# Layer 2's shift and scale as VectorE sums, attention's list in a new order, scaling shared with GpSimd

## The chip, the cores and the metric

The kernel runs on one core of a Trainium2 chip. The engines that matter are TensorE (PE, with its weight loads as PEld), VectorE (DVE), ScalarE (ACT), GpSimd (POOL) and SyncE (SP), which issues most of the loads. Each engine takes its instructions in order and waits on semaphores for the others. The metric is the device time of one execution in microseconds, as the median of several runs; beside it stands one execution that the hardware profiler recorded.

## The reference

Two layers on 256 tokens of width 1024, in float32. Each layer is `x + gate * mixer(rmsnorm(x, g) * (1 + scale) + shift)`, and shift, scale and gate are thirds of one product with the condition vector c (1024 numbers):

```
for i in range(DEPTH):
    shift, scale, gate = jnp.split(c @ ada_w[i] + ada_b[i], 3, axis=-1)
    h = rmsnorm(x, norm_g[i]) * (1.0 + scale[:, None, :]) + shift[:, None, :]
    y = nsa_mixer(h, ...) if i == 0 else mlstm_mixer(h, ...)
    x = x + gate[:, None, :] * y
return rmsnorm(x, final_g)
```

Layer 1's mixer is sparse attention: 16 heads in 4 groups, a compressed, a selected and a sliding branch (with 256 tokens the selected and the sliding branch see all earlier tokens), each a softmax with a distance bias, weighted by sigmoid gates, multiplied by a SiLU path z and projected by w_out. Layer 2's mixer is a chunkwise mLSTM. Shift and scale of layer 2, 2 x 1024 sums over the 1024 entries of c, are what the change computes in another way. They depend on c and weights alone and are needed first when layer 2 begins.

## The kernel before

**Stages.** The opening norms the tokens, makes layer 1's shift and scale and projects the queries and the compression inputs (up to about 50 us); eight blocks of key, value and gate weights follow (to 71 us); then come the attention (71 to about 158 us), its output projection with the residual, the norm of layer 2 (the boundary, `turn`, to about 195 us), and layer 2.

**Weights.** All weights go through one queue: `add` enters a block, `_load_one` issues its DMA on SP, in the queue's order, into one of ten buffers called raw. A block's buffer is free for the tenth block behind it once it was used. Weights that TensorE multiplies are split into two float32r parts, the high part by ACT (`make_hi`, L162) and the rest by DVE (`make_lo`, L167), the steps `hi` and `lo`; others (kind None) are used as they are, through `take_raw`.

**The attention's list.** Between 71 and 158 us nothing is left to a scheduler. `ORDER` is a text of some 300 steps, and each engine gets its instructions in the order in which the steps issue them. A step names its kind and numbers. n = 0 to 7 counts pairs of key groups: four heads i = n // 2, two group pairs n % 2.

- `S:n,a` scores on PE (L770, L773), `m:n,a` adds distances and takes minima on DVE (L787, out of PSUM into a tile Pr), `e:n,a` exponentials on ACT (L794), `f:n` factors from sums and gates on DVE (L800 to L802).
- `s:n,j` and `p:n,j` scale the four pieces of one Pr by the factors (L808), s on DVE, p on POOL; `T:n,j,br` turns a third of them on PE (L813), `t:n,j,br` copies the turned ones on ACT (L641, into PT), `V:n` multiplies by the values on PE (L830), `C:i` adds the compressed branch (L835), `y:i` multiplies by z on DVE (L839), `Y:i` splits that in two (ACT L641, DVE L843).
- `z:n,q` are quarters of the SiLU path's products (L1598 to L1600), `zt`, `zo` its tanh and product; `hidden:n`, `gelu`, `turned`, `second`, `ckeys`, `cscores`, `cexp` and others are the compressed branch; `gr`, `gc`, `gs`, `ga` layer 1's gate.
- `cr:n` makes a quarter of layer 2's shift and scale as rows: 32 small matmuls on PE (`ada_rows`, L224), which leave four partial sums on four rows per 32 partitions; `cc` copies them out of PSUM on ACT; `cs` (`ada_sums`) turns the copy by four transposes on PE (L1617), adds the four parts on DVE (L1620) and applies bias and norm weight (L1627, L1628). Three quarters stand in the list, the fourth in `turn` at the boundary.

In the opening, layer 1's own shift and scale are made another way: `columns` (L416) multiplies a block of 128 weight rows, laid out with the outputs on partitions, by a broadcast c (`cbc`, 128x1024) on DVE and sums along the row in the same instruction.

**The boundary.** `turn` finishes the output projection (L878, last parts), applies the residual (`residual`, L1070 and L1071), squares on ACT (L1106), makes the root (`rms_rsqrt`, L207 to L212), scales (L1110, L1111), turns the rows (`transposed`, L1120) and applies shift and scale (`modulate`, L1130, L1132).

Of the kernel before, what the change touches and what calls it, by code (L numbers as in the profile page):

```python
# [23 lines left out]
class Kernel:  # L24
# [223 lines left out]
    def setup(self):  # L248
# [25 lines left out]
        c = self.compress = self.T(self.p1, [P, 704])  # L274
# [12 lines left out]
        self.dc = self.T(self.p1, [P, 2, 4, 4, 16])  # L287
        slopes = self.T(self.p1, [P, 16])
# [32 lines left out]
    def layer1(self):  # L321
# [32 lines left out]
        for n in range(4):  # L354
            hidden(n)

        def gate_path(ih, gp):
            for k in range(2):
                self.add("z", [P, 4, 2, 128], t["path"][4 * ih + 2 * gp + k])

        self.gate_path = gate_path
# [8 lines left out]
    def first_phase(self, place):  # L370
# [8 lines left out]
        self.cbc = self.T(pc, [P, D], tag="gate")  # L379
# [59 lines left out]
        def parameters():  # L439
            nc.vector.tensor_scalar(pca[:, 80:88], pca[:, 80:88], 1.0, None, op0=OP.add)  # L440
# [120 lines left out]
    def nsa(self, acc):  # L561
# [4 lines left out]
        self.gate0, self.cols1 = self.T(pc, [P, D], tag="gate"), []  # L566
# [56 lines left out]
    hi hidden:0 bias hi hidden:1 S:0,0 S:0,1 hidden:2 lo m:0,0 e:0,0 hidden:3 m:0,1 lo e:0,1 gelu:0 f:0 gelu:1 S:1,0 s:0,0 gelu:2 z:0,0 z:0,1 s:0,1 params  # L623
    T:0,0,0 hi T:0,0,1 turned S:1,1 m:1,0 t:0,0,0 second t:0,0,1 z:0,2 T:0,1,0 e:1,0 z:0,3 ckeys m:1,1 t:0,1,0 e:1,1 cvalues:0 cscores:0 lo cscores:1 zt:0
    f:1 p:1,0 T:0,1,1 cvalues:1 ccopy:0 S:2,0 ccopy:1 t:0,1,1 S:2,1 V:0 m:2,0 T:1,0,1 T:1,0,0 ctokens:0 e:2,0 zo:0 m:2,1 t:1,0,1 cdist:0 ctokens:1 t:1,0,0
    hi cdist:1 cexp z:1,0 e:2,1 p:1,1 T:1,1,1 lo cprobs z:1,1 cparts:0 cparts:1 T:1,1,0 z:1,2 z:1,3 S:3,0 zt:1 t:1,1,0 f:2 S:3,1 t:1,1,1 m:3,0 s:2,0
    cturned:0 zo:1 cpt:0 e:3,0 V:1 cturned:1 C:0 m:3,1 y:0 T:2,0,1 t:2,0,1 T:2,0,0 t:2,0,0 p:2,1 gr:0 cpt:1 T:2,1,0 T:2,1,1 e:3,1 t:2,1,0 t:2,1,1 gc:0 f:3
    S:4,0 gr:1 s:3,1 V:2 m:4,0 gs:0 s:3,0 ga:0 gc:1 hi S:4,1 T:3,0,1 m:4,1 T:3,0,0 gs:1 hi hi ga:1 t:3,0,1 t:3,0,0 T:3,1,1 e:4,0 lo e:4,1 T:3,1,0 t:3,1,0
    S:5,0 m:5,0 hi f:4 p:4,0 t:3,1,1 S:5,1 s:4,1 C:1 z:2,0 z:2,1 m:5,1 e:5,0 lo cr:0 V:3 T:4,0,1 z:2,2 T:4,0,0 t:4,0,1 e:5,1 T:4,1,1 z:2,3 y:1 t:4,0,0
    cc:0 lo f:5 t:4,1,1 zt:2 T:4,1,0 t:4,1,0 S:6,0 S:6,1 m:6,0 zo:2 V:4 s:5,0 m:6,1 T:5,0,0 p:5,1 z:3,0 e:6,0 T:5,0,1 e:6,1 t:5,0,1 lo cs:0 f:6 t:5,0,0  # L630
    z:3,1 cr:1 Y:0 T:5,1,0 T:5,1,1 cc:1 s:6,1 S:7,0 t:5,1,1 S:7,1 s:6,0 t:5,1,0 V:5 m:7,1 T:6,0,1 T:6,0,0 z:3,2 hi e:7,1 z:3,3 m:7,0 lo cs:1 e:7,0 t:6,0,0
    t:6,0,1 T:6,1,0 f:7 zt:3 zo:3 C:2 t:6,1,0 hi hi y:2 T:6,1,1 t:6,1,1 cr:2 cc:2 hi V:6 cs:2 lo out:0 lo root s:7,1 Y:1 hi out:1 lo p:7,0 lo hi lo Y:2
    """

    def attention(self, hidden_block):
# [31 lines left out]
        def turned():  # L667
# [3 lines left out]
            hk = W["hk"] = T([P, 2, 64])  # L671
            hv = W["hv"] = T([P, 2, 4, 2, 16])
# [131 lines left out]
        def scaled(n, j, e):  # L804
# [878 lines left out]
```

## Time and profile before

| | |
|---|---|
| median of 3 runs | 436.75 us (436.2 to 436.87) |
| profiled execution, own time | 436.06 us |
| its span in the trace | 434.0 us |
| mean granted TensorE clock | 0.997 |
| attention, weights of layer 2's shift and scale | 16 loads of 512 KB |

The page of the profile has six parts: busy time by engine, the span in 40 slices, DMA queues, the chain of work that ended last, the costliest groups of instructions and the DMA issues. Besides it the trace answers queries: busy times in windows, groups by line, what an engine waited for, the chain in order of time, and a timeline. In a group's row, `x128 | 7.7, 382 | 0.0` is the count, the busy time in us, the mean of one in ns, and the idle time ahead; a row of the timeline or the chain starts with its start and its length in us; a row of waits ends with the sum, the number and the longest. "DVE y L658 <- PE bank L590" reads: DVE's instruction of line 658, which writes a tile y, waited for PE's of line 590, which wrote a bank of PSUM.

### The profile page before, as it was taken

Reading aid. Unit: us, or ns where it says so; the run is one execution under the profiler, and the core shown is the slowest. Engines: PE = TensorE matmul, PEld = TensorE weight load, DVE = VectorE, ACT = ScalarE, POOL = GpSimd, SP = SyncE. Lnnn points to the kernel's source line nnn. Section 1 sums busy time; section 2 is a strip of 40 time slices with the busy share of each in tenths; the row PEclk is TensorE's granted clock in tenths of the full one; section 3 lists DMA queues with packets and bytes.
Section 4 is the critical chain, followed back from the end, with each engine's and each line's share of the span. In section 5 each row is a group of like instructions: output and inputs, shape, how many; then the busy total and the mean of one; then the engine's idle time right before and its main releaser. Section 6 shows DMA issues by size and latency. Waiting matters only on the chain.

```text
span 434.0 us, 7874 instructions
## 1 busy us (share of the span) xinstructions
PE 425.4 (98%) x2864; PEld 365.7 (84%) x2864; DVE 336.5 (78%) x751; ACT 272.7 (63%) x544; POOL 37.5 (9%) x92
## 2 busy tenths in 40 slices
PE   8999999999999999999999999999999999999994
PEld 4999998888688777888999899988888888888883
DVE  5999897889677596879985497889887977458554
ACT  6665785777976974659476765564466455455522
POOL 4000302152032200120000000000000000000000
PEclk9999999999999999999999999999999999999998
DMA  8999986931875698638764456638555867540002
GB/s 325 416 415 418 401 264 190 400 143 51 311 297 191 251 337 271 243 97 267 267 189 151 148 164 198 203 131 275 194 153 194 277 248 218 182 136 0 2 0 97
DMA packets 26886, 94.55 MB, mean 218 GB/s; under 512 B 3072, under 2 KB 3088, under 8 KB 26848
## 3 DMA queue, kind: packets, MB, share of 16 engines
q1 hardware_dynamic: 26208, 92.30, 60.8%
q10 hardware_dynamic: 288, 0.79, 0.7%
q0 software_dynamic: 352, 0.97, 0.7%
q8 instruction: 22, 0.36, 0.3%
q14 instruction: 16, 0.13, 0.1%
HBM read 93.00 MB, written 1.05 MB: 217 GB/s over the span
## 4 chain that ended last, share of the span: by engine, by line
PE 94%; DVE 2%; DMA 1%; ACT 1%; issue 1%; SPq 0%; DVEq 0%
PE bank L559 10%; PE bank L557 10%; PE bank L558 10%; PE bank L452 8%; PE bank L1600 6%; PE bank L1599 6%; PE bank L1598 6%; PE bank L878 5%; PE bank L1509 5%; PE bank L1039 5%; PE bank L1153 4%; PE bank L224 3%; PE bank L830 3%; PE bank L813 3%; PE bank L1389 2%; PE bank L770 2%
## 5 line engine op out<-in xcount | busy, mean ns | idle before, releaser
L167 DVE TENSOR_TENSOR wl<-raw,wh 128x1024 fp32r<-128x1024 f32 (+4 forms) x127 | 137.3, 1099 | 39.8 <-ACT wh L162 37.7
L162 ACT ACTIVATE wh<-raw 128x1024 fp32r<-128x1024 f32 (+4 forms) x127 | 119.0, 958 | 72.9 <-PE bank L559 30.3
L557 PE MATMUL bank<-wh,one 128*128 128x512 f32 (+1 forms) x208 | 76.8, 370 | 0.0
L559 PE MATMUL bank<-wh,one 128*128 128x512 f32 (+1 forms) x208 | 76.3, 368 | 0.0
L558 PE MATMUL bank<-wl,one 128*128 128x512 f32 (+1 forms) x208 | 76.3, 367 | 0.0
L1598 PE MATMUL bank<-one,wh 128*128 128x256 f32 x208 | 59.6, 286 | 0.0
L1600 PE MATMUL bank<-one,wl 128*128 128x256 f32 x208 | 59.3, 285 | 0.1
L1599 PE MATMUL bank<-one,wh 128*128 128x256 f32 x208 | 59.0, 284 | 0.0
L559 PEld LDWEIGHTS bank<-wh,one 128*128 128x128 f32 x208 | 39.2, 188 | 6.1
L557 PEld LDWEIGHTS bank<-wh,one 128*128 128x128 f32 x208 | 39.2, 188 | 6.1 <-DVE tz L529 0.2
L558 PEld LDWEIGHTS bank<-wl,one 128*128 128x128 f32 x208 | 39.2, 189 | 6.0
L1600 PEld LDWEIGHTS bank<-one,wl 128*128 128x128 f32 x208 | 39.7, 191 | 0.5 <-DVE wl L167 0.3
L1599 PEld LDWEIGHTS bank<-one,wh 128*128 128x128 f32 x208 | 39.8, 191 | 0.1
L1598 PEld LDWEIGHTS bank<-one,wh 128*128 128x128 f32 x208 | 39.8, 191 | 0.1
L452 PE MATMUL bank<-one,wh 128*128 128x256 f32 x224 | 29.7, 283 | 0.0
L794 ACT ACTIVATE Pr<-Pr,mn 128x128 f32<-128x128 f32 (+1 forms) x64 | 28.2, 447 | 1.8 <-DVE mn L787 1.7
L452 PEld LDWEIGHTS bank<-one,wh 128*128 128x128 f32 x224 | 28.1, 192 | 0.0
L808 POOL TENSOR_SCALAR Pr<-Pr,f 128x128 f32<-128x128 f32 (+1 forms) x24 | 18.8, 801 | 47.9 <-DVE f L802 34.9
L1370 DVE SCALAR_TENSOR_TENSOR conv<-bank,one,conv 128x255 f32<-128x255 f32 (+2 forms) x48 | 20.2, 472 | 2.1 <-ACT conv L1365 2.1
L787 DVE CUSTOM_DVE_ANT_0 Pr<-bank,one 128x128 f32<-128x128 f32 (+1 forms) x64 | 18.8, 351 | 3.3 <-PE bank L773 2.1
L641 ACT ACTIVATE PT<-bank 128x384 f32<-128x384 f32 x32 | 14.6, 487 | 8.2 <-PE bank L813 8.2
L878 PE MATMUL bank<-wh,Q 128*128 128x512 f32 x48 | 16.7, 406 | 0.0
(341 smaller groups left out, 785.0 us busy)
## 6 DMA issues: line engine op xcount, KB each, us to landing
raw<-in_wide SPq DMA_DIRECT2D x44, 512.0 KB, 4.3
raw<-in_units SPq DMA_DIRECT2D x18, 512.0 KB, 3.6
raw<-in_gates SPq DMA_DIRECT2D x16, 512.0 KB, 5.4
raw<-in_turn SPq DMA_DIRECT2D x16, 512.0 KB, 5.7
raw<-in_out_b SPq DMA_DIRECT2D x16, 512.0 KB, 3.8
raw<-in_start SPq DMA_DIRECT2D x8, 512.0 KB, 9.5
Q<-in_columns SPq DMA_DIRECT2D x8, 512.0 KB, 9.6
raw<-in_hidden SPq DMA_DIRECT2D x8, 512.0 KB, 4.7
```

The costliest lines, as they stand in the source:

```text
L162: self.nc.scalar.activation(v(hi), src, AF.Copy)
L167: self.nc.vector.tensor_sub(v(lo), src, v(hi).bitcast(F32))
L452: nc.tensor.matmul(out, w[:, ch * P : ch * P + P], h[:, kk], start=(kk == 0 and m == 0 and ch % 2 == 0), stop=(kk == 7 and m == 2), skip_g ...
L557: nc.tensor.matmul(out, self.hh[:, kk, sl], wh, start=first, stop=False, skip_group_check=True)
L558: nc.tensor.matmul(out, self.hh[:, kk, sl], wl, start=False, stop=False, skip_group_check=True)
L559: nc.tensor.matmul(out, self.hl[:, kk, sl], wh, start=False, stop=last, skip_group_check=True)
L794: nc.scalar.activation(v, v, AF.Exp, bias=mn[:, a, br, j : j + 1], scale=-1.0, accum_out=sm[:, a, br, j : j + 1])
L878: nc.tensor.matmul(out, l[:, sl], w[:, c0:c1], start=(k == 0 and m == 0), stop=(k == 7 and m == 2), skip_group_check=True)
L1039: ins = nc.tensor.matmul(out, l[:, sl], w[:, c0:c1], start=(k == 0 and m == 0), stop=(k == N - 1 and m == 2), skip_group_check=True)
L1598: nc.tensor.matmul(out, wh, self.hh[:, kk], start=first, stop=False, skip_group_check=skip)
L1599: nc.tensor.matmul(out, wh, self.hl[:, kk], start=False, stop=False, skip_group_check=skip)
L1600: nc.tensor.matmul(out, wl, self.hh[:, kk], start=False, stop=last, skip_group_check=skip)
```

## The change

Layer 2's shift and scale no longer pass through TensorE. A new step `d:s,n` takes one block of 128 outputs and does on DVE what `columns` does in the opening: one multiply-and-sum over 1024 elements with the broadcast c, which also applies bias and norm weight. Sixteen of them take the place of `cr`, `cc`, `cs` and of the fourth quarter in `turn`. `cbc` gets a tile of its own, since it now lives to the end of the attention, and the weights are laid out anew.

The list is rewritten as a whole. Sixteen `d` are spread over it, from its first step to its last; a step `q` is new, which gives one branch of a scaling to DVE and the other to POOL. Of the sixteen scalings, ten were `s` and six `p`; now three are `s`, eight `p` and five `q`. The weights' queue is built from the list itself, in the order of first use. Pr is allocated at the minima and no longer at the scores, and PT has eight buffers in place of four.

```
-        for n in range(4):
-            hidden(n)
...
-        self.cbc = self.T(pc, [P, D], tag="gate")
+        self.cbc = self.T(p1, [P, D])
...
-            nc.vector.tensor_scalar(pca[:, 80:88], pca[:, 80:88], 1.0, None, op0=OP.add)
+            nc.vector.scalar_tensor_tensor(pca[:, 80:88], pca[:, 80:88], 1.0, pca[:, 64:72], op0=OP.add, op1=OP.mult)
...
-        F = self.F[n, o] = self.T(self.p1, [P, 8, 4, 16], tag="PT", bufs=4)
+        F = self.F[n, o] = self.T(self.p1, [P, 8, 4, 16], tag="Pr", bufs=4)
...
-    hi hidden:0 bias hi hidden:1 S:0,0 S:0,1 hidden:2 lo m:0,0 e:0,0 hidden:3 m:0,1 lo e:0,1 gelu:0 f:0 gelu:1 S:1,0 s:0,0 gelu:2 z:0,0 z:0,1 s:0,1 params
+    d:0,0 hidden:0 hi hidden:1 bias S:0,0 lo S:0,1 hi hidden:2 hidden:3 z:0,0 m:0,0 m:0,1 e:0,0 lo S:1,0 e:0,1 f:0 gelu:0 s:0,0 hi S:1,1 gelu:1
...
-            _, mn, _, bx, by = st[n]
+            Pr, mn, _, bx, by = st[n]
+            if not Pr:
+                Pr.extend(T([P, 2, 384], tag="Pr", bufs=4) for _ in range(2))
...
-        def scaled(n, j, e):
+        def scaled(n, j, *es):
             for br in range(2):
                 for a in range(2):
                     v = probs(n, j, br, a)
-                    e.tensor_scalar(v, v, F[n][:, a, br, j : j + 1], None, op0=OP.mult)
+                    es[br].tensor_scalar(v, v, F[n][:, a, br, j : j + 1], None, op0=OP.mult)
...
-            pt = PT[n, j, br] = T([P, 384], tag="PT", bufs=4)
+            pt = PT[n, j, br] = T([P, 384], tag="PT", bufs=8)
...
+        def column(s, n):
+            if not n:
+                self.cols1[s] = self.T(pc, [P, 4], tag="cols1", bufs=4)
+            b, kc, raw = n // 2, 2 * s + n % 2, self.take_raw(1)[0]
+            scale = self.pca[:, 64 + kc : 65 + kc] if b else 1.0
+            nc.vector.tensor_tensor_reduce(raw, raw, self.cbc, scale, self.pca[:, 72 + 8 * b + kc : 73 + 8 * b + kc], OP.mult, OP.add, self.cols1[s][:, n : n + 1])
...
-        def cols_sum(s):
-            self.cols1.append(self.ada_sums(W["A"], 64, 72, 80, s, 3, "cols1", 2))
...
-               "s": lambda n, j: scaled(n, j, nc.vector), "p": lambda n, j: scaled(n, j, nc.gpsimd),
+               "s": lambda n, j: scaled(n, j, nc.vector, nc.vector), "p": lambda n, j: scaled(n, j, nc.gpsimd, nc.gpsimd), "q": lambda n, j: scaled(n, j, nc.vector, nc.gpsimd),
...
+        for name in self.ORDER.split():
+            w, _, args = name.partition(":")
+            args = [int(x) for x in args.split(",")] if args else []
+            if w == "hi":
+                high()
+                his += 1
+            elif w == "hidden":
+                self.hidden_stream(*args)
+            elif w == "d":
+                self.add(None, [P, D], t["turn"][2 * args[0] + args[1] % 2, args[1] // 2])
+            elif w == "gr":
+                self.gate_stream(0, *args)
...
         square(0, 0)
-        bank = self.bank(6)
         square(0, 1)
-        self.ada_rows(bank, self.take_raw(4))
-        A = self.T(pc, [P, 512], tag="adaA", bufs=2)
-        nc.scalar.activation(A, bank, AF.Copy)
         for half in range(2):
             last(1, half, [4, 5])
         scale(0)
         lo(3)
-        self.cols1.append(self.ada_sums(A, 64, 72, 80, 3, 6, "cols1", 2))
         transposed(0)
```

Three places in the built programs show what moved. In them `raw` is a loaded block, `wh`, `wl`, `KL`, `KH` are split weights, `Q` holds queries and later the gated outputs, `one_44` and `one_41` are c in two layouts, and `cols` the shift and scale columns.

On PE at the boundary of the program before, between the end of the first token half's projection and that of the second, stands the last row product:

```order
L878 MATMUL bank_2250<-KH_2254,Q_1020 128x512 x3
L224 MATMUL bank_2432<-raw_2218,one_44_146 32x256 x2
L224 MATMUL bank_2432<-raw_2220,one_44_146 32x256 x2
L224 MATMUL bank_2432<-raw_2218,one_44_146 32x256 x2
L224 MATMUL bank_2432<-raw_2220,one_44_146 32x256 x2
L224 MATMUL bank_2432<-raw_2222,one_44_146 32x256 x2
L224 MATMUL bank_2432<-raw_2247,one_44_146 32x256 x2
L224 MATMUL bank_2432<-raw_2222,one_44_146 32x256 x2
L224 MATMUL bank_2432<-raw_2247,one_44_146 32x256 x2
L878 MATMUL bank_2251<-wh_2278,Q_965 128x512
```

At the same place of the changed program PE goes from one half to the other, and from there to the turns of the normalized rows (its lines are numbered 3 to 7 higher):

```order
L881 MATMUL bank_2109<-KH_2113,Q_1018 128x512 x3
L881 MATMUL bank_2110<-wh_2175,Q_963 128x512
L881 MATMUL bank_2110<-wl_2176,Q_963 128x512
L881 MATMUL bank_2110<-wh_2175,Q_963 128x512
L881 MATMUL bank_2110<-wh_2199,Q_963 128x512
L881 MATMUL bank_2110<-wl_2200,Q_963 128x512
```

Eight rows of two matmuls each are gone (the trace counts a float32 matmul twice here, so they are 32 there), and with them the four transposes ahead of L1120.

On DVE, at the end of the list and the first steps behind it, the program before has splits, scaling and rests:

```order
L167 TENSOR_TENSOR wl_2225<-raw_2104,wh_2224 128x1024
L167 TENSOR_TENSOR wl_2279<-raw_2106,wh_2278 128x1024
L167 TENSOR_TENSOR wl_2304<-raw_2108,wh_2303 128x1024
L843 TENSOR_TENSOR Q_965<-y_442_2187,Q_965 128x512
L167 TENSOR_TENSOR KL_2253<-raw_2214,KL_2253 128x1024
L167 TENSOR_TENSOR KH_2254<-raw_2216,KH_2254 128x1024
L839 TENSOR_TENSOR y_486_2369<-bank_2227,xT_1183 128x512
```

The changed one has two column sums (L864) at the list's end, ahead of the two splits for the projection's last parts:

```order
L167 TENSOR_TENSOR wl_2176<-raw_1898,wh_2175 128x1024
L167 TENSOR_TENSOR wl_2200<-raw_1985,wh_2199 128x1024
L841 TENSOR_TENSOR Q_963<-y_451_2209,Q_963 128x512
L864 ISA raw_2012,cols_435_2151<-raw_2012,one_41_147,one_8_70 128x1024
L864 ISA cols_435_2151 128x1
L864 ISA raw_2081,cols_435_2151<-raw_2081,one_41_147,one_8_70 128x1024
L864 ISA cols_435_2151 128x1
L167 TENSOR_TENSOR KL_2112<-raw_2138,KL_2112 128x1024
L167 TENSOR_TENSOR KH_2113<-raw_2203,KH_2113 128x1024
L837 TENSOR_TENSOR y_474_2307<-bank_2229,xT_1128 128x512
```

The two sums have moved in between the last rest of a gated output and the splits of KL and KH.

On DVE in the middle of the list, behind the minima of n = 5, the program before scaled and split; the factors f of the next pair follow at once:

```order
L167 TENSOR_TENSOR wl_1711<-raw_1457,wh_1710 128x4x128 x2
L839 TENSOR_TENSOR y_379_1890<-bank_1658,xT_1183 128x512
L167 TENSOR_TENSOR wl_1715<-raw_1638,wh_1714 128x4x128 x2
L800 TENSOR_SCALAR f_1900<-sm_1749 128x8
L801 RECIPROCAL f_1900<-f_1900 128x8
L802 TENSOR_TENSOR f_1900<-f_1900,one_177_831 128x8
```

In the changed one two column sums stand between the same kinds of steps, while POOL scales both halves of n = 4:

```order
L864 ISA raw_1686,cols_315_1610<-raw_1686,one_41_147,one_8_70 128x1024
L864 ISA cols_315_1610 128x1
L167 TENSOR_TENSOR wl_1759<-raw_1464,wh_1758 128x4x128 x2
L864 ISA raw_1690,cols_315_1610<-raw_1690,one_41_147,one_8_70 128x1024
L864 ISA cols_315_1610 128x1
L167 TENSOR_TENSOR wl_1834<-raw_1688,wh_1833 128x4x128 x2
L936 SCALAR_TENSOR_TENSOR xT_1128<-zb_1854,bank_1723 128x2x256
L798 TENSOR_SCALAR f_1915<-sm_1714 128x8
```

What moved: two sums have come in ahead of the factors of n = 5, and the scaling that follows f of n = 4 has left DVE.

More of the change, by code (lines that the diff above doesn't have):

```diff
@@ L273, in setup @@
             nc.vector.memset(self.sel[32 * j : 32 * j + 1], 1.0)
-        c = self.compress = self.T(self.p1, [P, 704])
+        early = self.T(self.p1, [P, 1216], tag="PcT")
+        c = self.compress = early[:, 512:1216]
         self.b1bc, self.b2v = c[:, 0:256], c[:, 256:320]
@@ L285, in setup @@
         g.affine_select(self.dm[:, 0], self.dm[:, 0], pattern=[[-1, SEQ]], compare_op=OP.is_ge, fill=64 * BIG, base=P, channel_multiplier=1)
-        self.dc = self.T(self.p1, [P, 2, 4, 4, 16])
-        slopes = self.T(self.p1, [P, 16])
+        self.dc = early[:, 0:512].rearrange("p (a i g s) -> p a i g s", a=2, i=4, g=4)
+        slopes = tokens[:, 1, D : D + 16]
         for i in range(16):
@@ L353, in layer1 @@
             self.add("s", [P, 816], t["keys"][kk])
-        for n in range(4):
-            hidden(n)
[L357 to L361, printed above, removed]
+        self.hidden_stream = hidden
         self.stream_rest()
@@ L633 @@
+    q:7,0 hi out:1 t:6,1,0 t:6,0,1 d:3,1 T:6,1,1 hi lo y:2 Y:1 t:6,1,1 lo root q:7,1 lo V:6 lo Y:2 d:3,2 d:3,3
     """
@@ L763, in scores @@
                 mn, sm = T([P, 2, 2, 2], tag="mn", bufs=3), T([P, 2, 2, 2], tag="sm", bufs=3)
-                st[n] = [T([P, 2, 384], tag="Pr", bufs=4) for _ in range(2)], mn, sm, bx, by
+                st[n] = [], mn, sm, bx, by
             bx, by = st[n][3:]
@@ L851, in rows @@
         def rows(what, n, bank):
[L852 removed]
+            b = self.bank(bank)
+            B.setdefault("ada", []).append(b)
             self.ada_rows(b, self.take_raw(4))
         def rows_copy():
[L856 to L857 removed]
+            A = self.T(pc, [P, 512], tag="adaA", bufs=2)
+            copy(A, B["ada"].pop(0))
+            W.setdefault("A", []).append(A)
+        def column(s, n):
[4 more added lines that the diff above has]
+            nc.vector.tensor_tensor_reduce(raw, raw, self.cbc, scale, self.pca[:, 72 + 8 * b + kc : 73 + 8 * b + kc], OP.mult, OP.add, self.cols1[s][:, n : n + 1])
         def gate_bias():
@@ L863, in gate_sum @@
             b = B["gs"] = self.bank(bank)
-            nc.tensor.matmul(b, self.sel, W["A"], start=True, stop=True)
+            nc.tensor.matmul(b, self.sel, W["A"].pop(0), start=True, stop=True)
         def gate_add(n):
@@ L886, in out_part @@
                     w = T([P, 2, 1024], F32R, tag=tag)
-                    self.spare[self.out1 + n] = [w[:, m] for m in range(2)]
+                    self.spare[self.outs[n]] = [w[:, m] for m in range(2)]
             w = self.take()
@@ L938, in stream_rest, with high @@
         t = self.t
-        self.gate_path(0, 0)
-        self.gate_path(0, 1)
-        for n in range(2):
-            self.gate_stream(0, n)
-        for gp in range(2):
-            self.gate_path(1, gp)
-        for s in range(3):
-            self.turn_stream(s)
-        self.out1 = len(self.queue)
-        for i in range(4):
-            for gp in range(2):
-                self.add("s", [P, 1024], t["out_a"][2 * i + gp])
-        self.turn_stream(3)
+        self.outs, his = [], 0
+        def high():
+            if his < 8:
+                self.add("z", [P, 4, 2, 128], t["path"][his])
+            else:
+                self.outs.append(len(self.queue))
+                self.add("s", [P, 1024], t["out_a"][his - 8])
+        for name in self.ORDER.split():
[10 more added lines that the diff above has]
+                self.gate_stream(0, *args)
+        for his in range(his, 16):
+            high()
         half = lambda c0, k: self.add("s", [P, 4, 256], t["units"][2 * min(c0 // 256, 8) + k])
@@ L988, in cols_stream @@
                 self.add(None, [P, KC, P], self.t["opening"][b])
-    def turn_stream(self, s):
-        for k in range(4):
-            self.add(None, [P, 4, 256], self.t["turn"][4 * s + k])
     def gate_stream(self, l, n):
@@ L1660, in layout @@
     out["columns"] = a["ada_w"][0][:, : 2 * D].reshape(D, 2, KC, P).transpose(2, 1, 3, 0)[1:]
-    out["turn"] = flat([modulation[1][:, 4 * h : 4 * h + 4, b, 256 * s : 256 * s + 256] for s in range(4) for b in range(2) for h in range(2)])
+    out["turn"] = a["ada_w"][1][:, : 2 * D].reshape(D, 2, KC, P).transpose(2, 1, 3, 0)
     out["gates"] = flat([ada[l][:, 2 * j : 2 * j + 2, 2 * D + 512 * n : 2 * D + 512 * n + 512] for l in range(2) for n in range(2) for j in range(4)])
```

33 lines of the change are left out of this document (15 added, 18 removed).

## The prediction

> **What bounds the kernel now.** I read the page first, for the busy time of the engines and the shares of the chain that ended last.
>
> ```profile
> PE 425.4 (98%) x2864; PEld 365.7 (84%) x2864; DVE 336.5 (78%) x751; ACT 272.7 (63%) x544; POOL 37.5 (9%) x92
> PE 94%; DVE 2%; DMA 1%; ACT 1%; issue 1%; SPq 0%; DVEq 0%
> ```
>
> TensorE carries 94% of the chain, so over the whole kernel a cut on it is a cut of the time. But the change lies in one stage, and there the question is who else is nearly full. The view by windows, cut to the stretch in which VectorE works through the attention's list (from its first step after the gates to the last Y:2), says:
>
> ```profile
> 73.60:160.80 87.20, 87.20 (x754) 69.14 (x751) 67.12 (x265) 69.23 (x209) 20.43 (x31) 1.00 0.67 246
> ```
>
> The columns are length, then PE, weight loads, DVE, ACT, POOL, then granted clock (1.00), DMA share and GB/s. PE is busy all 87.2 us; DVE 67.1, so it has 20.1 us of idle time. What it waited for is the list of DVE's waits in the same stretch:
>
> ```profile
> DVE cols L1620 <- PE bank L1617: 5.1, 2, 2.6
> DVE f L800 <- ACT Pr L794: 4.5, 4, 2.4
> ...
> DVE y L658 <- PE bank L590: 1.0, 1, 1.0
> ...
> DVE tz L724 <- PE bank L719: 0.7, 1, 0.7
> DVE adaA L745 <- ACT adaA L641: 0.5, 1, 0.5
> DVE one L691 <- PE bank L684: 0.3, 1, 0.3
> ```
>
> All its rows add up to 18.6 us; the other 1.5 are gaps too short to be listed. Most of the waits are for a TensorE that is late.
>
> **What TensorE loses.** The four row products form one group, and the chain shows what a product and its turn really take of the path (a group's mean counts the overlapped ends of matmuls twice):
>
> ```profile
> L224 PE MATMUL bank<-raw,one 128*32 128x256 f32 x128 | 7.7, 382 | 0.0
> 172.49 1.86 PE bank L224 x32
> ...
> 177.34 0.44 PE bank L1617 x4
> 177.78 0.87 PE bank L1120 x8
> ```
>
> Each product is 32 matmuls in 1.86 us, each turn 0.44, so 4 x 2.30 = **9.2 us** of TensorE go: 6.9 inside the attention, 2.3 at the boundary between the layers. Nothing is added on TensorE. That is the most the change can bring.
>
> **What VectorE gains.** The new sum is an operation that this kernel already runs, in the opening, at L416: the same 1024 elements times the same broadcast c.
>
> ```profile
> L416 DVE CUSTOM_DVE_ANT_0 Q<-Q,gate,one 128x1024 f32<-128x1024 f32 x8 | 10.2, 1310 | 0.2 <-DMA Q<-in_columns 0.2
> 113.25 1.00 DVE L808 TENSOR_SCALAR Pr<-Pr,f 128x128 f32<-128x128 f32 x4
> 148.71 2.99 POOL L808 TENSOR_SCALAR Pr<-Pr,f 128x128 f32<-128x128 f32 x4 [15.48 <-DVE f L802]
> 147.36 0.17 DVE L1620 TENSOR_REDUCE cols<-bank 128x4 f32<-128x16 f32 x1 [2.58 <-PE bank L1617]
> 147.57 0.23 DVE L1627 TENSOR_TENSOR cols<-cols,one 128x2 f32<-128x2 f32 x2
> 147.83 0.16 DVE L1628 TENSOR_TENSOR cols<-cols,one 128x2 f32<-128x2 f32 x1
> ```
>
> By the busy time of its group one sum is 10.2 / 8 = 1.27 us, so 16 are +20.3 us. A scaling set (four operations) is 1.00 on DVE and 2.99 on POOL; the list before has ten sets on DVE and six on POOL, the new one three on DVE, eight on POOL and five halved, so DVE loses 4.5 sets, -4.5 us, and POOL goes from 18 to 8 x 2.99 + 5 x 1.50 = 31.4 us. The small sums behind the turns go: three in this stretch at 0.56, -1.7 us. DVE's work in the list becomes 67.1 + 20.3 - 4.5 - 1.7 = **81.2 us**, on an engine that starts it at 73.6: it cannot end before 154.8, where it ended at 160.8. TensorE's side, 6.9 us less, would end its list at about the same distance earlier. So the engine with idle time becomes one with hardly any, and the sum has to be made on VectorE.
>
> **From VectorE's end to the boundary.** What follows the list there is fixed work in a row:
>
> ```profile
> 160.76 1.22 DVE L167 TENSOR_TENSOR KL<-raw,KL 128x1024 fp32r<-128x1024 f32 x1
> 161.90 1.22 DVE L167 TENSOR_TENSOR KH<-raw,KH 128x1024 fp32r<-128x1024 f32 x1
> 164.19 0.69 DVE L839 TENSOR_TENSOR y<-bank,xT 128x512 f32<-128x512 f32 x1 [1.08 <-PE bank L835]
> 165.58 0.69 DVE L843 TENSOR_TENSOR Q<-y,Q 128x512 fp32r<-128x512 f32 x1 [0.70 <-ACT Q L641]
> 166.36 2.56 DVE L167 TENSOR_TENSOR wl<-raw,wh 128x816 fp32r<-128x816 f32 x3
> 171.16 0.69 DVE L1070 TENSOR_TENSOR y<-bank,gate 128x512 f32<-128x512 f32 x1 [2.24 <-PE bank L878]
> ...
> 173.26 0.69 DVE L1071 TENSOR_TENSOR one<-one,y 128x512 f32<-128x512 f32 x1
> 174.61 0.58 ACT L1186 ACTIVATE adaA<-bank 128x512 f32<-128x512 f32 x1
> 176.19 0.72 ACT L1110 ACTIVATE Pr<-one,rq_y 128x512 f32<-128x512 f32 x1 [0.82 <-DVE rq_y L212]
> ```
>
> Without the two waits for PE (1.08 and 2.24, which vanish if DVE is the late one): the two splits 2.36, y 0.69, ACT's copy 0.70, its rest 0.69, three splits 2.56, four residual operations 171.16 to 173.95 = 2.79, and the norm to the end of L1110 at 176.91, 2.96, less about 0.5 because the copy at L1186 stood between the squares and the root on ACT and is gone. Together 12.2 us from the end of the list to the turn of the normalized rows at L1120, which starts at 177.78 before. So with w for all DVE idle and lost time inside the list, that turn starts at 154.8 + w + 12.2 = 167.0 + w, and **the gain is 10.8 - w**, at most 9.2. Before, w was 20.1. Behind this point the instructions of every engine stand as before but for line numbers, PE is unbroken there in the chain, and a gain made here stays.
>
> **What w will be.** Three parts.
> First, the 1.5 us of short gaps stay.
> Second, waits for a result that was only just made. The 5.1 for the turns go with them, and those for scores shrink, since DVE comes to the scores later. Of the 4.5 for ACT's exponentials most go, because in three of four places a column sum or a split now stands ahead of the factors; I keep one, 1.1. The early waits have nothing new ahead of them: 1.0 (the hidden product), 0.7, 0.5 and 0.3, so 2.5. One new wait: only four Pr buffers exist, and m:5,0 now stands before the turns T:3,1,x are over; I take the 0.7 of L724, another wait for a few turns. Sum 4.3. Bounds: nearly nothing if TensorE is always ahead (1.5), and 9 if all waits for ACT and half of those for PE stay.
> Third, POOL. Before, its work met a DVE split in only one place:
>
> ```profile
> 124.03 1.43 POOL L808 TENSOR_SCALAR Pr<-Pr,f 128x256 f32<-128x256 f32 x1
> 130.82 0.92 POOL L808 TENSOR_SCALAR Pr<-Pr,f 128x256 f32<-128x256 f32 x1
> 124.05 1.49 DVE L167 TENSOR_TENSOR wl<-raw,wh 128x512 fp32r<-128x512 f32 x2
> 118.31 1.29 DVE L167 TENSOR_TENSOR wl<-raw,wh 128x512 fp32r<-128x512 f32 x2
> 124.05 0.69 DVE L167 TENSOR_TENSOR wl<-raw,wh 128x512 fp32r<-128x512 f32 x1
> ```
>
> POOL's operation grew by 0.51, the pair of splits by 0.20 in 1.4 us side by side: 0.14 us of DVE per us. No row shows a column sum beside POOL; like a split it has two inputs in SBUF, so I take the same price. Sums (20.3) and splits (17.6, sixteen halves and six or more whole ones) are 37.9 us of DVE time, POOL is at work in 31.4 of 87 us, so about 13.7 us meet, at 0.14 that is 1.9. Bounds: 0, and 6.3 if each of the 38 operations that meets POOL (36%) waits for half of a 0.92 operation.
> So w = 1.5 + 4.3 + 1.9 = 7.7 and the gain 10.8 - 7.7 = **3.1 us**.
>
> The Trainium skill, page SBUF — State Buffer, section Who interferes with whom, says that VectorE and GpSimd share one port pair as an exclusive lock, held for the whole instruction, so that the loser blocks fully. The rows agree only in part: POOL lost about what the split lasted, but the first split took an undisturbed 0.69 though POOL's operation had started 0.02 before it. By the page's rule the third part would be nearer the 6.3, and the gain 10.8 - 12.1 = -1.3; it is a rival below.
>
> **Edits at no cost.** The weights of the sums are the same 16 loads of 512 KB, moved into the order of use on SP's queue, ten slots deep, with the DMAs at 0.67 of their time. One place is tight: the last block of hidden weights now takes the slot of the first column sum.
>
> ```profile
> 46.40 17.84 SPq L86 DMA_DIRECT2D raw<-in_hidden x8
> raw<-in_hidden SPq DMA_DIRECT2D x8, 512.0 KB, 4.7
> 76.55 3.60 PE bank L590 x32
> ```
>
> All eight were issued by 64.2. Now the eighth waits for a sum that ends at about 74.9, and lands 4.7 later, at 79.6, where hidden:3 would start at 76.55 + 1.8 = 78.3. This can cost TensorE 1.3 us at a place where DVE waits too (the 1.0 above). I count none of it extra, since TensorE catches up while DVE is the late one; without that cover it is up to 1.3. POOL's longer sets, up to 6 us in a row behind the fourth factors, have over 8 us of TensorE work ahead of the turns that need them. The eight PT buffers only remove waits of ACT; the broadcast c in its own tile, slopes, compress and hk, hv in other tiles move no instruction.
>
> **The rivals.**
> 1. TensorE stays the bound: DVE's order has work ready at every wait, w is 2 to 4, gain 7 to 9, median near 428.6. For it: no wait of PE itself is listed in this stage before. Against: 81 us of DVE work in 87 less 9 us leaves nothing for a hop between engines.
> 2. The port: column sums and GpSimd's scaling stop each other. Price 6.3 or more in place of 1.9, and POOL's 31 us grow by as much as they meet, so that late turns of Pr hold TensorE as well: w of 12 to 14, 1 to 3 us slower, about 438.7. It decides from the point where POOL costs DVE over 10.8 - 1.5 - 4.3 = 5.0 us, that is 0.36 us for each of some 14 meetings (36% of 38 operations); the rows show 0.1 to 0.2.
> 3. The front: hidden weights land late, second waits for hk and hv behind a split, and the list starts 1.5 to 3 us behind on both engines. Gain 0 to 1.4, about 436.
> That the products do not leave TensorE is excluded: the built order has none of them.
>
> **How the numbers follow.** The profiled execution took 436.06 (span 434.0), 0.7 under the median of 436.75; the gain is taken off the median: 436.75 - 3.1 = 433.65, **433.7 us**. Chances: the forecast (gain 0.8 to 6.5) 0.56, rival 1 0.15, rival 2 0.17, rival 3 0.12. The range leaves out the outer ends of rivals 1 and 2: 429.5 to 438.2. A measurement tells about 0.2%, 0.87 us, from no change: faster 0.53 + 0.15 + 0.03 = 0.71, the same 0.12, slower 0.17.
>
> **What would show it.** In the same stretch of the new profile DVE should be busy about 83 us and over 90%, PE should have lost 6.9 us of matmuls and show first waits for DVE in the attention, and DVE's two waits for PE behind the list (1.08, 2.24) should be gone. The column sums should read 1.27 to 1.5 us. PE without a wait and DVE with 8 us or more of idle time would make rival 1 right; sums of 1.6 us and POOL sets of 5 us rival 2. The forecast is wrong if the turn at the boundary does not start at about 175.

## The result and the profile after

The changed kernel takes **430.65 us** (median of 4 runs, 430.04 to 430.79) against 436.79 for the kernel before in the same runs (436.20 to 436.87): the ratio is 0.9860, with a 95% interval of 0.9843 to 0.9877. That is 6.1 us off, where the prediction had 3.1. The profiled execution took 430.58 (span 428.7).

The page of the changed kernel, engines and chain:

```profile
PE 416.9 (97%) x2720; PEld 360.8 (84%) x2720; DVE 350.2 (82%) x749; ACT 271.0 (63%) x540; POOL 65.6 (15%) x110
PE 83%; DVE 7%; DMA 4%; ACT 3%; issue 1%; SPq 0%; DVEq 0%; ACTq 0%
```

TensorE has 144 records fewer (four products of 32, four turns of 4) and 8.5 us less busy time. The chain now runs for 7% over VectorE, where it was 2%: those pieces stand between 104 and 137 us, where the chain leads from sums, minima and factors on VectorE over exponentials on ScalarE to TensorE. The view by windows, from the first step of VectorE's list (the sum of d:0,0) to the end of its last sum, shows how full it is (columns as in the prediction: length, PE, weight loads, DVE, ACT, POOL, clock, DMA share, GB/s):

```profile
74.35:159.43 85.08, 83.92 (x671) 67.49 (x668) 81.61 (x266) 69.24 (x208) 48.73 (x50) 1.00 0.76 271
```

VectorE is busy 81.61 of 85.08 us, 96%, and TensorE 83.92. Both are nearly full. What each waited for there and up to the boundary, first VectorE's waits in that stretch, then TensorE's from 70 to 200 us (us in total, times, longest):

```profile
DVE y L653 <- PE bank L584: 1.0, 1, 1.0
...
DVE f L798 <- ACT Pr L792: 0.8, 2, 0.5
DVE adaA L670 <- PE bank L665: 0.3, 1, 0.3
DVE tz L720 <- PE bank L715: 0.2, 1, 0.2
```

```profile
PE bank L1127 <- ACT Pr L1117: 1.3, 1, 1.3
PE bank L584 <- DMA raw<-in_hidden: 0.8, 1, 0.8
PE bank L811 <- ACT PT L636: 0.3, 1, 0.3
```

The kernel before had no wait of TensorE in this part. Now there are three, and none of them names VectorE, though by the chain the shortest, for ScalarE's copy (L636) at 137 us, leads back through VectorE's list to 104 us. The largest stands at the boundary; the chain of the changed kernel, from the end of the list to the turn of the normalized rows, shows how it comes about (start, length, what):

```profile
159.80 6.98 PE bank L881 x30
...
166.81 0.70 DVE y L1077
...
167.53 0.69 DVE one L1078
168.22 0.67 DVE y L1077
...
168.91 0.70 DVE one L1078
...
171.50 0.73 ACT Pr L1117
...
172.27 1.09 PE bank L1127 x8
```

Up to 166.8 the chain is TensorE's own projection; from there the residual, the squares, the root and the scaling take 5.5 us, in which TensorE has only the other half's products to do. Last, the sums and GpSimd's scalings (busy, mean ns):

```profile
L806 POOL TENSOR_SCALAR Pr<-Pr,f 128x256 f32<-128x256 f32 x21 | 28.4, 1351 | 0.0
L864 DVE CUSTOM_DVE_ANT_0 raw<-raw,one,one 128x1024 f32<-128x1024 f32 x16 | 21.1, 1331 | 0.0
L806 POOL TENSOR_SCALAR Pr<-Pr,f 128x128 f32<-128x128 f32 x21 | 19.0, 906 | 31.9 <-DVE f L800 28.4 <-ACT PT L636 3.5
```

**Where the time went.** A measure that all runs below share is S, the time from TensorE's first hidden product to its turn of the normalized rows at the boundary. Its two ends before, and its start after (the end is the 172.27 above), by TensorE's timeline:

```profile
71.28 1.08 PE L590 MATMUL bank<-raw,PT 128*64 128x256 f32 x8
...
177.61 1.04 PE L1120 MATMUL bank<-one,Pr 128*128 128x128 f32 x8
```

```profile
72.12 1.08 PE L584 MATMUL bank<-raw,Pr 128*64 128x256 f32 x8
```

S was 106.3 and is 100.2: 6.2 us less, and behind the turn both profiles take the same (256.3 and 256.5). That is the whole gain. The start itself is 0.84 later in the profile after; it is no effect of the change, since two runs below (e4 and e9) with the opening of before started at 71.25 and at 72.17.

### The profile page after: what moved, and what is told of

Same layout as the page of the kernel before. It is cut to its first block, busy times and chain, and to the rows that moved or that the text cites. A ratio compares the mean times of both kernels' runs of the same rounds, so it can differ in the third digit from the quotient of the medians.

```text
span 428.7 us, 7633 instructions
## 1 busy us (share of the span) xinstructions
PE 416.9 (97%) x2720; PEld 360.8 (84%) x2720; DVE 350.2 (82%) x749; ACT 271.0 (63%) x540; POOL 65.6 (15%) x110
## 4 chain that ended last, share of the span: by engine, by line
PE 83%; DVE 7%; DMA 4%; ACT 3%; issue 1%; SPq 0%; DVEq 0%; ACTq 0%
PE bank L553 10%; PE bank L551 10%; PE bank L552 10%; PE bank L446 8%; PE bank L1602 5%; PE bank L1601 5%; PE bank L1600 5%; PE bank L1511 5%; PE bank L1046 5%; PE bank L881 4%; PE bank L1160 4%; PE bank L1391 2%; ACT Pr L792 2%; DVE wl L167 2%; DMA raw<-in_hidden 1%; DMA raw<-in_opening 1%
## 5 line engine op out<-in xcount | busy, mean ns | idle before, releaser
L806 POOL TENSOR_SCALAR Pr<-Pr,f 128x128 f32<-128x128 f32 (+1 forms) x42 | 46.8, 1129 | 31.9 <-DVE f L800 28.4
L864 DVE CUSTOM_DVE_ANT_0 raw<-raw,one,one 128x1024 f32<-128x1024 f32 x16 | 21.1, 1331 | 0.0
```

The lines of the kernel that those rows point to most:

```text
L806: es[br].tensor_scalar(v, v, F[n][:, a, br, j : j + 1], None, op0=OP.mult)
```

## The experiments

Two theories stood against each other. **D**: VectorE's list now sets the end, as the prediction says, and TensorE follows it. **T**: TensorE still sets it, and what is missing from the 9.2 us are the single waits above. (Some expectations write E for a milder D: VectorE stands just at its edge, so what is added to it counts in full and what is taken from it does not.) All runs were timed against the kernel before on the same chip; "behind" is the time from the turn at the boundary to the end of the trace. S and "behind" come from one profiled execution of each kernel. The seven whose part behind the turn is the same differ there by 0.13 at most, so a difference of 0.1 or 0.2 in S says nothing.

| run | median us | ratio to before, 95% | S | behind |
|---|---|---|---|---|
| before | 436.79 | | 106.3 | 256.3 |
| changed | 430.65 | 0.9860 (0.9843 to 0.9877) | 100.2 | 256.5 |
| e1: sums cut to 16 columns | 430.02 | 0.9841 (0.9827 to 0.9854) | 99.3 | 256.4 |
| e2: four sums made twice | 435.58 | 0.9966 (0.9954 to 0.9979) | 105.0 | 256.5 |
| e3: GpSimd's scalings left out | 429.92 | 0.9840 (0.9826 to 0.9854) | 99.8 | 256.4 |
| e4: before, turns gone | 435.37 | 0.9962 (0.9950 to 0.9975) | 104.6 | 256.7 |
| e9: before, products gone too | 432.17 | 0.9891 (0.9878 to 0.9905) | 101.4 | 256.8 |
| e5: sums in the old order | 443.80 | 1.0158 (1.0144 to 1.0172) | 112.5 | 258.0 |
| e6: all scaling on VectorE | 437.22 | 1.0009 (1.0000 to 1.0018) | 106.6 | 256.5 |
| e8: boundary in another order | 432.17 | 0.9885 (0.9870 to 0.9901) | 100.7 | 257.5 |
| e10: e8, two roundings later | 429.88 | 0.9841 (0.9827 to 0.9855) | 98.9 | 257.5 |
| e7: first sum behind hidden | 430.21 | 0.9851 (0.9837 to 0.9865) | 99.7 | 256.5 |
| e12: e10 and e7 | 429.66 | 0.9836 (0.9822 to 0.9850) | 98.3 | 257.6 |
| e13: e12, one split later | 429.57 | 0.9833 (0.9820 to 0.9847) | 98.3 | 257.2 |

### Less and more work on VectorE: e1 and e2

In e1 each sum covers 16 of the 1024 columns:

```diff
-  nc.vector.tensor_tensor_reduce(raw, raw, self.cbc, scale, ...)
+  nc.vector.tensor_tensor_reduce(raw[:, 0:16], raw[:, 0:16], self.cbc[:, 0:16], scale, ...)
```

> The changed kernel with the 16 column sums cut to 16 of their 1024 columns, so that VectorE loses 16 x about 1.2 = 19 us in the attention and everything else stays. Theory D (VectorE's list sets the end): TensorE's waits in this part (0.98 for the hidden weights, 0.51, and 1.49 for the norm at the boundary) all go, so 2.5 to 3 us faster than the changed kernel, about 427.8. Theory T (TensorE still sets it; the wait for the norm is there because the boundary's product and turn had covered the norm's latency and are gone): only the hidden weights' wait goes, because the first sum frees its slot 1.2 us earlier; 1 us faster at most, about 429.7, and the wait of TensorE for ACT's normalized rows, about 1.3, is still listed.

In e2 the second sum of each group of four is followed by another:

```diff
+  if n == 1:
+      nc.vector.tensor_tensor_reduce(raw, raw, self.cbc, 1.0, 0.0, OP.mult, OP.add, self.cols1[s][:, 2:3])
```

> The changed kernel with four of the 16 sums made twice (the second of each group of four, its second result overwritten later): VectorE has 4 x 1.3 = 5.2 us more work in the attention. Theory D: VectorE was busy 96% there, with 2.3 us of waits that could take some of it: 3.5 to 5 us slower than the changed kernel, 434 to 435.7. Theory T: TensorE's queue has slack against VectorE, at most 1.5 us slower, 432 or less.

e1 took 17 us of busy time off the sums (21.1 to 4.3) and shortened S by only 0.8. TensorE's waits in e1, and one of VectorE's:

```profile
PE bank L1127 <- ACT Pr L1117: 1.3, 1, 1.3
PE bank L584 <- DMA raw<-in_hidden: 0.6, 1, 0.6
```

```profile
DVE y L1077 <- PE bank L881: 2.2, 1, 2.2
```

The wait for the norm is there as before, with VectorE waiting 2.2 us for TensorE ahead of the residual. So at the boundary TensorE is the one that sets the end: T. But e2, with 5.3 us more on VectorE, lengthened S by 4.9, and there TensorE does wait for VectorE:

```profile
PE bank L828 <- DVE y L837: 1.6, 1, 1.6
PE bank L811 <- DVE Pr L806: 1.6, 3, 0.6
```

Both halves are needed: D alone misses e1, T alone misses e2. The changed kernel stands where the two engines' limits nearly meet. VectorE has some 0.4 us to spare (5.3 less 4.9, and its wait for TensorE ahead of the residual is 0.38), and freeing it altogether brings 0.8.

### The price of GpSimd: e3 and e6

e3 leaves out the scalings that stand on GpSimd; e6 puts them all on VectorE (each p and q of ORDER becomes an s).

```diff
   for br in range(2):
+      if es[br] is nc.gpsimd:
+          continue
```

> The changed kernel with the scalings that stand on GpSimd left out (those on VectorE stay), so that GpSimd is silent in the attention. By the durations in the changed kernel's trace (sums 1331 ns instead of 1310 in the opening, half-block splits 708 instead of 697) GpSimd costs VectorE about 1 us: 0 to 1 us faster, 429.7 to 430.6, sums back to 1310 ns. Port rival: waits for the lock that the durations don't show cost VectorE 4 us or more: the time falls by all that VectorE can give, 2.5 to 3 us, to about 427.8.

```diff
-  ... p:0,1 ... q:1,0 ... p:1,1 ...
+  ... s:0,1 ... s:1,0 ... s:1,1 ...
```

> The changed kernel with every scaling on VectorE: 8 sets of 1.0 us and 5 halves of 0.5 more on it, 10.5 us, and GpSimd silent. Theory E: at its edge VectorE has some 0.5 to 2 us to take it up, and gets back about 1 us for GpSimd's absence: 7 to 9 us slower than the changed kernel, 438 to 440. Port rival: what VectorE loses to GpSimd comes back, so 3 us slower at most, 433.6 or less.

e3: S is 0.3 shorter, the median not distinguishable from that of the changed kernel. By itself that says little about the port, since e1, with 17 us less on VectorE, brought just as little. The durations show what GpSimd costs VectorE. VectorE's own scalings by windows from 74 to 160 us, in the changed kernel (with GpSimd's busy time behind them) and in e3, and the sums in e3:

```profile
74.00:160.00 86.00, 7.02 (x22) 46.76 (x42) 1.00 0.76 270
```

```profile
74.00:160.00 86.00, 5.74 (x22) 1.00 0.76 275
```

```profile
L866 DVE CUSTOM_DVE_ANT_0 raw<-raw,one,one 128x1024 f32<-128x1024 f32 x16 | 20.7, 1310 | 0.0
```

The 22 scalings cost 1.3 us more beside GpSimd, the 16 sums 0.4, and the twenty 512-wide splits 0.4 (13.3 against 12.9 busy): 2.1 us in all. Beside GpSimd's 46.76 us of work the longest of the 16 sums took 1.48 and the shortest 1.27, so none stood still for the length of a GpSimd operation (0.6 us at least). A wait that the durations do not show would have to lie in VectorE's short gaps, 85.08 less 81.61 less the 2.3 of listed waits, that is 1.2 us. With that GpSimd costs VectorE 3.3 us at most, and the port rival, 4 us or more, is refuted. e6 is 6.5 us slower than the changed kernel, under the 7 to 9 of theory E and far over the 3 of the rival. VectorE takes 42 scalings more at 0.25 each (10.5 us), gets 2.1 back because GpSimd is silent, and had 0.4 to spare; that would make 8.0, so 1.5 us of what it was spared stay unnamed. Sharing the scalings is worth 6.5 us to this order.

### TensorE's part by itself: e4 and e9

In the kernel before, each product keeps 4 of its 16 matmuls (one for each block, so that buffers come free in order), and its turn, copy and small sums are left out (shift and scale of layer 2 are a constant):

```diff
-  self.ada_rows(b, self.take_raw(4))
+  raws = self.take_raw(4)
...
+  for r, raw in enumerate(raws):
+      nc.tensor.matmul(b[0:32, 256 * (r // 2) : ...], self.crep[:, 0], raw[:, 0], ..., tile_position=(0, 0))
```

> The kernel before with its four row products cut to 4 of their 32 matmuls each, and their turns, copies and small sums left out: TensorE's part of the change by itself, in the old order, with nothing added. If all that leaves TensorE counts: 8.9 us faster (9.2 less 16 matmuls), 427.9. If the boundary's product covered the norm's latency (theory T): about 1.3 of it come back as a wait of TensorE for ACT before the turns at the boundary, 429.2. If VectorE in the old order cannot follow either, there are waits of TensorE for VectorE in the attention and it is slower than that.

This missed: 1.6 us faster where 7.6 to 8.9 was expected. TensorE's timeline in e4 has the reason:

```profile
122.96 1.91 PE L858 MATMUL bank<-raw,one 128*32 128x256 f32 x8
```

The 4 matmuls (8 records) take 1.91 us, as the 32 records did in the kernel before (1.86 on the path). The 16 stand in four column groups, four matmuls in each; since all 16 took as long as the four of one group, the groups ran side by side, and a product is four steps long with 16 matmuls and with 4. e4 removed only the turns: 4 x 0.44 = 1.8 us, and S fell by 1.7. e9 makes the four matmuls 8 columns wide:

```diff
-  ... b[0:32, 256 * (r // 2) : ...], self.crep[:, 0], raw[:, 0], ...
+  ... b[0:32, 8 * r : 8 * r + 8], self.crep[:, 0], raw[:, 0, 0:8], ...
```

> Second try at TensorE's part by itself. In the first try the 4 matmuls left of each product took 1.91 us, as the 16 had (four column groups run side by side), so only the turns were really gone. Now each of the 4 reads 8 columns in place of 256, so that the 7.4 us of the products go too. If all that leaves TensorE counts in the old order: 436.96 - 9.2 + 0.3 = 428.1. Theory T (the boundary's product covered the norm's latency): 1.3 come back as TensorE's wait for ACT's normalized rows, 429.4. If the old order holds TensorE up at other places once the products are gone: slower than 430, and the waits of TensorE name them.

```profile
123.88 0.42 PE L858 MATMUL bank<-raw,one 128*32 128x8 f32 x8
```

```profile
PE bank L1127 <- ACT Pr L1117: 0.8, 1, 0.8
PE bank L830 <- DVE y L839: 0.7, 1, 0.7
PE bank L813 <- POOL Pr L808: 0.4, 1, 0.4
```

The products now take 0.35 of the path, so 4 x 1.5 + 1.8 = 7.8 us are gone from TensorE, and S fell by 4.9. Of the 2.9 that did not arrive 1.9 are these three waits: the norm's, as T says, and two for GpSimd's scalings and VectorE's gating that the old order has ready too late once TensorE is faster. Some 1 us is left unnamed. So in the old order the ceiling of 9.2 us does not hold even with nothing put on VectorE.

### The order: e5

The table of before, with the sums where the small sums behind a turn stood, and before's ten and six scaling sets:

```diff
-  ... cr:0 ... cc:0 ... cs:0 ...
+  ... d:0,0 d:0,1 d:0,2 d:0,3 ...
```

> The changed kernel's sums and tiles in the order of before, with its sharing of the scalings (ten sets on VectorE, six on GpSimd): the four sums of a group stand together where the small sums behind the turn stood, the last four at the end of the list. VectorE's work in the list is 67.1 + 20.3 - 1.7 = 85.7 us in place of 81.2. Theory E (VectorE is at its edge: what is added to it counts in full, what is taken from it does not): the turn at the boundary comes some 4 us later than in the changed kernel, 434 to 436. Theory T with slack: 432 or less. If the groups of four in a row (5.2 us) hold TensorE up as well: 436 or more.

It is 13 us slower than the changed kernel and 7 slower than before: not the 434 to 436 of VectorE's added work alone, but the last case, in which the groups of four hold TensorE up as well. TensorE's waits, and VectorE's timeline at the longest of them:

```profile
PE bank L827 <- DVE y L836: 4.1, 1, 4.1
PE bank L810 <- DVE Pr L805: 3.4, 1, 3.4
PE bank L1126 <- ACT Pr L1116: 2.6, 1, 2.6
```

```profile
150.00 1.35 DVE L863 CUSTOM_DVE_ANT_0 raw<-raw,one,one 128x1024 f32<-128x1024 f32 x1
...
151.27 1.35 DVE L863 CUSTOM_DVE_ANT_0 raw<-raw,one,one 128x1024 f32<-128x1024 f32 x1
...
153.85 0.69 DVE L836 TENSOR_TENSOR y<-bank,xT 128x512 f32<-128x512 f32 x1
```

Four sums in a row stand ahead of the gating y (L836) that TensorE needs next, and it waits 4.1 us. TensorE then paid a second time. Here are the windows from the first matmul behind each of the three waits (columns as above, the clock third from the end):

```profile
144.20:149.00 4.80, 4.80 (x29) 4.78 (x30) 4.80 (x21) 4.31 (x18) 0.00 (x0) 0.68 0.40 148
...
154.60:158.50 3.90, 3.90 (x21) 2.62 (x22) 3.90 (x7) 3.55 (x6) 3.24 (x3) 0.63 0.95 362
...
184.70:189.00 4.30, 4.28 (x16) 3.75 (x17) 2.71 (x7) 2.97 (x6) 0.00 (x0) 0.60 0.35 123
```

The granted clock was 0.68, 0.63 and 0.60 there, and 1.00 from 158.5 to 184.7 us. An estimate from these rows (length times what is missing from 1.00) is 1.5, 1.4 and 1.7 us: some 3 of the 12.4 us of S, and the 258.0 "behind", where the last of them falls. In the changed kernel, with waits of 1.3 at most, the clock reads 1.00 from 72 us to the turn; in e8, below, it reads 1.00 behind a wait of 1.7.

So with before's order, its sharing of the scalings and the sums in groups of four the change loses. Single sums in that order were not tried.

### The remaining waits: e8, e10, e7, e12, e13

e8 puts two products of row half 1 behind half 0's last ones, and the splits of two narrow weights and one wide one behind the residual and the norm:

```diff
-  for n in range(3): split(n)
-  for a in range(2):
-      for half in range(2): last(a, half, [3])
+  split(0); hi(1); hi(2)
+  for half in range(2): last(0, half, [3])
...
   square(0, 1)
+  lo(1)
+  for half in range(2): last(1, half, [3])
...
   scale(0)
-  lo(3)
+  lo(2)
...
   rest(0, 0)
+  lo(3)
```

> The changed kernel with the boundary written in another order: the two products of row half 1 with output weight 3 (2 x 0.69 us on TensorE) stand behind those of half 0 in place of ahead of them, and VectorE splits two of the three narrow weights and the first wide one behind the residual and behind the norm in place of ahead of them. So half 0's sums are complete 1.4 us earlier, and TensorE has 1.4 us more to do while the norm is made. Theory T (TensorE waits 1.3 there because the cover is gone): the wait goes, 1 to 1.3 us faster than the changed kernel, 429.4 to 429.7. If VectorE is late there in any case (its splits only move behind the norm): the wait turns up again at the first products of layer 2, and the time stays within 0.3 us.

It was 1.5 us slower. ScalarE's timeline in e8:

```profile
168.34 1.06 ACT L162 ACTIVATE wh<-raw 128x1024 fp32r<-128x1024 f32 x1 [3.08 <-issue]
169.31 0.61 ACT L1113 ACTIVATE Pr<-one 128x512 f32<-128x512 f32 x1
```

The sums of half 0 were complete 1.3 us earlier, but the rounding of a wide weight stood ahead of the squares on ScalarE and idled 3 us. The trace names no releaser; the postponed products, which read the buffer that this rounding takes over, end at about that time. e10 puts that rounding behind the norm:

```diff
-  hi(3)
   square(0, 0)
...
   scale(0)
+  hi(3)
...
-  hi(4)
   rounded(0)
+  hi(4)
```

> The boundary's other order a second time. In the first try half 0's sums were complete 1.3 us earlier as meant (VectorE's residual at 165.51 in place of 166.81), but ScalarE's first rounding of a wide weight stood ahead of the squares on its queue and had to wait until 168.34 for the buffer of output weight 3, whose last products the new order had put off. Now that rounding stands behind the norm, and the next one behind the rounding of half 0's rows. Theory T: TensorE's wait of 1.3 for the norm goes, and the time falls by 0.8 to 1.3 us against the changed kernel, 429.4 to 429.9. If the norm is late for another reason, or layer 2's first products now wait for the weights that are split later: within 0.3 us of the changed kernel, and the wait stands ahead of layer 2's products.

```profile
166.80 0.63 ACT L1113 ACTIVATE Pr<-one 128x512 f32<-128x512 f32 x1 [1.77 <-DVE one L1078]
```

```profile
PE bank L584 <- DMA raw<-in_hidden: 0.9, 1, 0.9
PE bank L1160 <- DVE one L1151: 0.7, 1, 0.7
PE bank L811 <- ACT PT L636: 0.4, 1, 0.4
```

The squares start at 166.80, the wait for the norm is gone, and S is 1.3 shorter, exactly that wait. But "behind" grew by 1.0, of which 0.7 is a new wait at layer 2's first products, for a remainder (L1151) behind the postponed split. In the median 0.8 us is left, which the intervals do not tell from nothing.

e7 moves the first column sum and its load behind the four hidden blocks:

```diff
-  d:0,0 hidden:0 hi hidden:1 ... f:0 gelu:0
+  hidden:0 hi hidden:1 ... f:0 d:0,0 gelu:0
```

> The changed kernel with the first column sum and its load behind the four hidden blocks in place of ahead of them (on VectorE behind the first factors), so that the eighth hidden weight no longer waits for that sum's slot. Theory T (TensorE alone sets the end): its wait of 0.8 to 1.1 for the hidden weights goes and the time falls by as much, 429.6 to 429.9. Theory E (VectorE is at its edge too): VectorE only trades its wait behind the first factors for one at the start of its list, so the time falls by 0.4 at most, 430.2 to 430.7, and TensorE's waits turn up later.

The wait for the hidden weights is gone, two of 0.2 for VectorE take part of its place, and S is 0.5 shorter. The 430.21 is what E expected (430.2 to 430.7) and not T's 429.6 to 429.9, though the intervals do not tell it from the changed kernel either. e12 joins e10 and e7; e13 also moves the wide split behind the second half's norm.

> Both of the two edits before together (boundary's other order, and the first column sum behind the hidden blocks). The boundary's order takes 1.7 us of splits out of VectorE's path to the norm, so VectorE has room there and the two gains should add up: 1.5 to 2.2 us faster than the changed kernel, 428.4 to 429.1. If one of the two edits does nothing alone, it does nothing here either.

```diff
   rest(0, 0)
-  lo(3)
...
   scale(1)
+  lo(3)
   lo(4)
```

> Both edits, with VectorE's split of the first wide weight put off once more, behind the norm of row half 1. In the runs with the boundary's other order that split (1.22 us) stood ahead of the second remainder of half 0's rows, and TensorE waited 0.7 for that remainder at layer 2's first products. Theory T: this wait goes too, 0.5 to 1.0 us faster than both edits alone (429.66), 428.7 to 429.2. If the split then comes late for its own products, TensorE waits at those by as much: 429.5 or more.

In S the two gains add up: 98.3, 1.9 under the changed kernel. TensorE's waits in e13:

```profile
PE bank L811 <- ACT PT L636: 0.5, 1, 0.5
PE bank L1160 <- DVE wl L167: 0.4, 1, 0.4
```

The postponed split now comes 0.4 late for its own products, and "behind" keeps 0.7 of what S gained. e12 and e13 both missed their forecasts (1.5 to 2.2, then 0.5 to 1.0 more): they are the fastest versions measured, 429.66 and 429.57, 1.0 to 1.2 us under the changed kernel by their ratios to before, with intervals that still touch its own. All of these keep the computation whole, as do e2, e5 and e6.

## Why the prediction was right, and where it was off

**Direction and mechanism.** VectorE was filled as forecast: 96% busy against "over 90%", the sums 1.33 us against 1.27 to 1.5, VectorE's two waits behind the list 0 and 0.38 in place of 1.08 and 2.24. e2 shows that its list does limit: added work comes out at the end nearly one to one. e5 shows that in the old order, grouped and with the old sharing, the 16 sums cost more than they bring. The gain was nearly twice the 3.1 forecast: the direction held by its mechanism, the size only because the main case (0.8 to 6.5) was wide.

**The size: w and its neighbours.** The forecast put the turn 101.1 us behind the list's start (81.2 work + 7.7 lost + 12.2 tail); it came at 172.27 - 74.35 = 97.9. Of the 9.2 us of TensorE's work 6.2 arrived. The 3.2 between forecast and result, term by term:

- Work and GpSimd's price together were put at 81.2 + 1.9 = 83.1 and measured 81.6. GpSimd's price was right in size (2.1 by e3), but in another place: it falls mostly on VectorE's scalings, which the prediction had not counted, and little on the sums and splits, which it had. The rest of the work was then some 1.7 smaller than reckoned.
- Waits for results just made were put at 4.3 and measured 2.3. Of the early ones those of 0.7 and 0.5 shrank or went, and the new one for a Pr buffer, put at 0.7, never came.
- Short gaps: 1.5 forecast, 1.2 measured (85.08 less 81.61 less 2.3). The tail: 12.2 forecast, 12.8 measured, in part because VectorE still waits 0.38 for TensorE in it.

So the mis-sized term is w, the time lost in VectorE's list: 7.7 forecast, 3.9 measured (85.08 less the forecast 81.2 of work). By the prediction's own mark, a turn at about 175, the forecast was too late by 2.7 us.

**Who sets the end.** The prediction had TensorE follow VectorE, with first waits for it in the attention. No such wait is listed (only the 0.3 that leads back to VectorE by the chain), and e1 shows that a VectorE with 17 us less to do brings only 0.8. Rival 1, TensorE as the bound, was nearer on this point, and its w of 2 to 4 too (3.9 measured); its 428.6 failed, because the **9.2 us ceiling** was wrong. That step counted the boundary's product and turn, 2.3 us, as pure gain. They had covered the norm's latency: taken away, 1.3 came back as a wait, which stays in e1 and goes in e10 when other products take the cover's place. The ceiling also fails in e9, where nothing was added to VectorE. In the changed kernel 2.4 of the 3.0 us that are missing from it are TensorE's three waits; 0.6 have no name.

**The hidden weights.** The prediction saw a wait of up to 1.3 and counted none, because TensorE could catch up while VectorE was late. It came, 0.8, and e7 got 0.5 of S by taking it away: half covered. The cause named was not quite right either. The chain of the changed kernel:

```profile
73.86 0.24 PE bank L584 x2
74.09 6.35 DMA raw<-in_hidden
80.49 1.94 PE bank L584 x14
```

The last hidden load is released by TensorE's own first hidden matmuls, not by the end of the sum at 75.6, and then takes 6.35 us rather than 4.7; so e1, with short sums, kept 0.6 of it.

**The port.** The rule weighed in the prediction (the Trainium skill, SBUF — State Buffer, section Who interferes with whom: an exclusive lock; that the loser blocks fully for the whole instruction the page says of VectorE's two-port modes) would have made the third part 6.3 us. VectorE lost 2.1. GpSimd lost far more: its 128x256 scaling went from the 0.92 us used in the prediction to 1.35, a set of four from 2.99 to 4.45 on average, and its work in the list was 46.8 us where 31.4 was reckoned. That is close to the POOL sets of 5 us that the prediction named as a sign of rival 2, but the sums did not come near its 1.6, and nobody waited for GpSimd (no wait of TensorE for it is listed). So the trace agrees that they contend, but the larger share of the price falls on GpSimd here.

## What to carry to other kernels

Work taken off the bounding engine gains at most what it did not cover: look which latency of other engines ran beside it, and put other work in its place. When work goes to the engine that was waiting, compare the two engines' busy time over the same stretch; once they meet, savings on either one alone bring almost nothing, while additions to one cost in full. And an order of instructions written by hand is made for its load: the changed kernel became 13 us slower when its sums stood in groups of four in the old order with the old sharing.

## What the runs showed of the hardware beside that

Four matmuls of 32 columns in one column group took 1.91 us, and sixteen in four groups 1.86 on the path: four groups cost nothing more than one, so removing three of four saves nothing. The Trainium skill, TensorE: Matmul & The Clock Gate, section Why this matters for your kernels, says likewise that outputs placed at different 32-partition groups run at the same time, and gives a speed-up of 2.38 for three of them; here four fitted in the time of one. In e5 the granted clock fell to 0.60 to 0.68 for some 4 us behind each of TensorE's waits of 2.6, 3.4 and 4.1 us, while behind waits of 1.3 (changed kernel) and 1.7 (e8) it stayed at 1.00. And a 128x1024 sum cut to 16 columns still took 282 ns of 1331 on VectorE (its group in e1: 16 in 4.3 us busy), so such an operation has a fixed part that small cuts do not touch.
